# An encoder block's feed-forward entry: gate sums in another pool, low parts on VectorE, one token sum left in its PSUM bank

## The chip, the cores and the metric

The kernel runs on one core of one Trainium2 chip. The metric is the device time of one execution in microseconds; the median of three runs stands for a kernel. One further execution was recorded by the hardware profiler. Engines are named as the profile names them: PE is TensorE, DVE is VectorE, ACT is ScalarE, POOL is GpSimd, SP is the engine whose queue issues the DMAs.

## The reference

One layer of an encoder over 1024 tokens and 16 meta tokens, width 1024, in float32:

```python
h = concatenate([meta, x])
h = h + mixer_block(rms_norm(h, norm_mix), ...)      # two attention branches, gated, times w_out
h = h + swiglu(rms_norm(h, norm_ffn), w_ff_gate, w_ff_up, w_ff_down)
return rms_norm(h, norm_final)[:, N_META:]

def swiglu(h, w_gate, w_up, w_down):                 # inner width 2816
    return (silu(h @ w_gate) * (h @ w_up)) @ w_down
```

The change lies where the mixer's output has just been added to h and `h @ w_gate` and `h @ w_up` begin.

## The kernel before

**Split operands.** Each float32 operand of a matmul is kept as two parts, high and low. `split` (L110 to L112) makes them: ScalarE copies the source to the high part (L111), and a chosen engine subtracts that from the source for the low part (L112). A product of two split operands is three matmuls per 128 rows of depth: high by high, high by low, low by high.

**Seven products in place of eight.** The products with the gate's and the up's weights are done blockwise, 2 by 2, with seven products p = 1 to 7 in place of eight. `fp` (0 to 10) counts blocks of 256 inner columns, `i` is 0 for the gate and 1 for the up. The tokens' operands are b11, b21, b22 and, made of sums, t_5, t_6, t_7 and t_4. The weights' operands are made by `weights` (L903 on): p = 1 and 2 need only a raw block, p = 6, 5, 7 and 3 also sums of raw blocks (L918 to L924). p = 4 uses a raw block.

**The order.** `order_f` starts with p = 1 and 2 of the first three blocks (`N_EARLY = 3`), twelve products that do not need the tokens' sums; then follow p = 6, 5, 7, 3, 4 of these blocks, and then blocks 3 to 10 in full. TensorE's order is as written. The order on the other engines in this part is set by a planner, which plays the program through in a model and takes what is ready, the earlier written first. It also chooses the buffers, PSUM banks included; each engine then works its queue in that order.

**Products and banks.** `product_f` runs one product of 12 matmuls into a PSUM bank. There are eight banks. The bank that p = 1 opens (`b1`) is kept for p = 6, 7 and 4 of the same (i, fp); p = 2 has a bank of its own for a short time, and p = 5 and 3 share one. After p = 1 ScalarE copies the bank to a tile of the pool of copies (`p_tile`, 7 buffers, L1110). After p = 2 VectorE adds that copy to the bank: for the gate into a new tile c (L1099), to which ScalarE applies SiLU (L1101), for the up into the copy itself (L1104), after which c is multiplied by it (L1106). Tiles c come from `c_tile`: from a pool `cpool` of eight buffers, once that is open, before that from the pool of copies. `cpool` and `spool` are put where the pool of the h2 tiles was (`close_h2`), and that closes once the last token sums are split.

**Tokens' sums.** `norm_f(t)` normalises 128 tokens, `turn_f(t)` transposes them into two banks and splits them. For t = 4 to 7 it also makes four sums with the kept tiles of t - 4, u = t - 4 (L1023 to L1026): t1, t2, and two made in place of the kept tile (`left`, `low`), both from t2. `split_t(u)` then splits the four sums into t_6, t_5, t_7 and t_4, the last with its low part on POOL. `turn_f(6)` and `turn_f(7)` stand at the steps n = 0 and 2 of the loop over the products (`TURN`), the splits at n = 1, 3, 3 and 4 (`SPLIT`).

**Ahead of the products.** `prepare` makes weights' operands up to eight ahead; they live in a ring of eight (`op_tile`). Raw blocks come through a ring of five (`raw_tile`), which the normalised tokens and the weights of w_out use too. All loads and stores are issued from SP's queue in the planner's order, the stores of the h2 tiles (L995) among them.

Of the kernel before, what the change touches and what calls it, by code (L numbers as in the profile page):

```python
# [13 lines left out]
ALU = mybir.AluOpType  # L14
# [55 lines left out]
def encoder_block(ctx: ExitStack, tc: tile.TileContext, x, meta, norm_mix, w_in, lq1, lk1, lq2, lk2,  # L70
                  subln, sink, w_ba, w_bb, w_o, norm_ffn, w_g, w_u, w_d, norm_final, out, dbg=None):
    nc = tc.nc
# [5 lines left out]
    def f32(ap):  # L78
        return ap.bitcast(F32)
# [30 lines left out]
    def split(hi, lo, src, lo_eng):  # L110
        nc.scalar.activation(hi, src, AF.Copy)  # L111
        lo_eng.tensor_tensor(lo, src, f32(hi), ALU.subtract)  # L112
# [326 lines left out]
    for i in range(2):  # L439
        cols = slice(960 * i, 960 * i + 960)  # L440
# [293 lines left out]
    def ps_bank(name):  # L734
        return bank(psum3, "bank", name, 8)
# [5 lines left out]
    def op_tile(name):  # L741
        return ring.tile([P, 2, 512], F32R, tag="op", name=name, bufs=OP_BUFS)

    def raw_tile(name):
        return ring.tile([P, 1024], F32, tag="raw", name=name, bufs=RING_RAW)
# [23 lines left out]
    for j in range(4):  # L769
        nc.sync.dma_start(tb[:, 4 + j, :], yb_d[j])  # L770
        yb_t.append(ybpool.tile([P, 2, S], F32R, name=f"yb{j}"))
        if j % 2:
            for h in range(2):
                cols = slice(h * 512, h * 512 + 512)
# [70 lines left out]
    def half_op(p, name):  # L845
        return p.tile([P, 2, 4, 512], F32R, name=name)

    def h2_tile(name):
        return h2pool.tile([P, D], F32, tag="h2", name=name, bufs=NT)
# [17 lines left out]
    first, rest, order_pm = (1, 2), (6, 5, 7, 3, 4), (1, 2, 6, 5, 7, 3, 4)  # L867
    N_EARLY = 3
# [25 lines left out]
    def load_unit(i, fp, ahead=None):  # L894

        src = (w_g, w_u)[i]
        if ahead is not None:
            w = ahead.rearrange("p (c n) -> p c n", n=P)
            nc.sync.dma_start(w, src[:, fp * 256:fp * 256 + P].rearrange("(c p) n -> p c n", p=P))
            raws[i, fp, 0], raws[i, fp, 1] = w[:, 0:4], w[:, 4:8]  # L900
            return
        for kh in range(2):
            w = raw_tile(f"wf{i}_{fp}_{kh}").rearrange("p (c n) -> p c n", n=256)  # L903
            nc.sync.dma_start(w, src[kh * 512:kh * 512 + 512, fp * 256:fp * 256 + 256].rearrange("(c p) n -> p c n", p=P))
            raws[i, fp, kh] = w

    def weights(i, fp, p):
        if (p == 1 and fp) or (p == 6 and fp < N_EARLY):
            load_unit(i, fp, raw_tile(f"wf{i}_{fp}") if p == 1 and fp < N_EARLY else None)
        nm = f"{i}_{fp}_{p}"  # L910
        tt = nc.vector.tensor_tensor
        a11, a12 = (raws[i, fp, kh][:, :, 0:P] for kh in range(2))
        a21, a22 = (raws[i, fp, kh][:, :, P:256] for kh in range(2)) if p not in first else (None, None)
        src = {1: a11, 2: a12, 6: a11, 7: a21, 3: a12, 4: a22}.get(p)
        if p == 6:

            s1 = temps[i, fp] = spools[0].tile([P, 4, P], F32, tag="s", name=f"s1_{nm}", bufs=S_TMP)
            tt(s1, a21, a22, ALU.add)  # L918
            tt(a21, a11, a21, ALU.subtract)
            tt(a11, s1, a11, ALU.subtract)  # L920
        elif p == 5:
            src = temps[i, fp]
        elif p == 3:
            tt(a12, a12, a11, ALU.subtract)  # L924
        op = op_tile(f"wop_{nm}").rearrange("p a (c n) -> p a c n", n=P)
        split(op[:, 0], op[:, 1], src, nc.gpsimd)
        return op

    wt, late, raws_d = {}, [], {}
# [54 lines left out]
    def four(t):  # L984
        return t.rearrange("p (c t) -> p c t", c=4)

    xns, sums_t, held = {}, {}, {}
# [10 lines left out]
    def turn_f(t):  # L998
        xn = xns.pop(t)
        half, u = divmod(t, 4)  # L1000
        cols = slice(u * P, u * P + P)
        pts = []
        kept = None if half else h2_tile(f"kept_{u}")
        for b in range(2):
            pt = four(ps_bank(f"ptn_f{t}_{b}"))
            for c in range(4):
                k = 4 * b + c
                nc.tensor.transpose(pt[:, c, :], xn[:, k * P:(k + 1) * P], ident)
            pts.append(pt)
            if b or not half:  # L1010
                op = b22 if half else (b11, b21)[b]
                nc.scalar.activation(op[:, 0, :, cols], pt, AF.Copy)
                nc.vector.tensor_tensor(op[:, 1, :, cols], pt, f32(op[:, 0, :, cols]), ALU.subtract)
            if not half:
                nc.scalar.copy(four(kept[:, b * 512:b * 512 + 512]), pt)
        if not half:
            held[u] = kept
            return

        kept, more = held.pop(u), h2_tile(f"ts_{u}")  # L1020
        left, low = four(kept[:, 0:512]), four(kept[:, 512:])
        t1, t2 = four(more[:, 0:512]), four(more[:, 512:])
        nc.vector.tensor_tensor(t1, pts[0], left, ALU.subtract)  # L1023
        nc.vector.tensor_tensor(t2, pts[1], t1, ALU.subtract)
        nc.vector.tensor_tensor(left, t2, left, ALU.subtract)
        nc.vector.tensor_tensor(low, low, t2, ALU.subtract)  # L1026
        sums_t[u] = {5: t1, 6: t2, 7: left, 4: low}

    for i in range(2):
# [32 lines left out]
    t_ops = {p: half_op(topool, f"t_{p}") for p in (5, 6, 7, 4)}  # L1062
# [4 lines left out]
    def p_tile(name):  # L1067
        return pcopy.tile([P, 512], F32, tag="pc", name=name, bufs=P_BUFS)

    def c_tile(name):  # L1070
        return cpools[0].tile([P, 512], F32, tag="c", name=name, bufs=C_BUFS) if cpools else p_tile(name)

    def split_t(u):
        cols = slice(u * P, u * P + P)
        for p in (6, 5, 7, 4):
            split(t_ops[p][:, 0, :, cols], t_ops[p][:, 1, :, cols], sums_t[u][p], nc.gpsimd if p == 4 else nc.vector)

    st = {}

    def product_f(fp, p, i):  # L1080
        op, b = ops.pop(("f", (fp, p, i))), b_ops[p]
        u = st.setdefault((i, fp), {})
        nm = f"{i}_{fp}"
        which = {1: "b1", 6: "b1", 7: "b1", 4: "b1", 2: "b2", 5: "b3", 3: "b3"}[p]
        if p in (1, 2, 5):
            u[which] = ps_bank(f"pg_{nm}_{p}")
        ps = u[which]
        for c in range(4):
            for n, (x, y) in enumerate(((0, 0), (0, 1), (1, 0))):
                nc.tensor.matmul(ps, op[:, x, c, :], b[:, y, c, :], start=(p in (1, 2, 5) and c == 0 and n == 0),  # L1090
                                 stop=(p in (4, 2, 3) and c == 3 and n == 2), skip_group_check=True)
        g = st.setdefault(("c", fp), {})

        def result(key, src, other=None):

            if i == 0:
                c = g[key] = c_tile(f"c_{nm}_{key}")
                if other is not None:
                    nc.vector.tensor_tensor(c, src, other, ALU.add)  # L1099
                    src = c  # L1100
                nc.scalar.activation(c, src, AF.Silu)  # L1101
            else:
                if other is not None:
                    nc.vector.tensor_tensor(other, src, other, ALU.add)  # L1104
                    src = other
                nc.vector.tensor_tensor(g[key], g[key], src, ALU.mult)  # L1106

        if p in (1, 5):
            u[p] = p_tile(f"p{p}_{nm}")
            nc.scalar.copy(u[p], ps)  # L1110
        elif p == 6:
            u[p] = p_tile(f"u2_{nm}")
            nc.scalar.copy(u[p], ps)
        elif p == 2:
            result("11", ps, u[1])
        elif p == 7:
            result("22", ps, u[5])
        elif p == 3:
            result("12", ps, u[6])
        else:  # L1120
            result("21", ps)
            if i:

                a11, a21, a12, a22 = g["11"], g["12"], g["21"], g["22"]
                nc.sync.dma_start(a_d[1][fp], a11)
                s1, s2, s3, s4 = (c_tile(f"as{k}_{fp}") for k in range(1, 5))
                nc.vector.tensor_tensor(s1, a21, a22, ALU.add)
                nc.sync.dma_start(a_d[4][fp], a22)
                nc.vector.tensor_tensor(s3, a11, a21, ALU.subtract)
                nc.sync.dma_start(a_d[7][fp], s3)  # L1130
                nc.vector.tensor_tensor(s2, s1, a11, ALU.subtract)
                nc.sync.dma_start(a_d[5][fp], s1)
                nc.sync.dma_start(a_d[6][fp], s2)
                nc.vector.tensor_tensor(s4, a12, s2, ALU.subtract)
                nc.sync.dma_start(a_d[2][fp], a12)
                nc.sync.dma_start(a_d[3][fp], s4)

    TURN, SPLIT = {0: 6, 2: 7}, {1: (0,), 3: (1, 2), 4: (3,)}
    for n in range(nf):
        prepare()  # L1140
        if n in TURN:
# [97 lines left out]
    for n in range(nf, len(steps)):  # L1239
        p, j = steps[n][1]  # L1240
# [3 lines left out]
        if p in LOADS:  # L1244
            at, half, col = LOADS[p]
            if at <= j < at + 4:
                t, cols = 4 * half + j - at, slice(col * 512, col * 512 + 512)
# [60 lines left out]
```

## Time and profile before

| | |
|---|---|
| median of three runs | 1465.75 us (1465.35 to 1465.88) |
| profiled execution, its own time | 1464.45 us |
| its span, first to last instruction | 1462.7 us |
| granted clock of TensorE, mean | 0.999 |
| TensorE matmul, busy | 1437.6 us, 98% |
| VectorE, ScalarE, POOL busy | 863.2, 660.3, 542.3 us |
| gate and up products on TensorE (L1090) | from 820.0 to about 1244 us |

A row of a timeline begins with its start in us from the span's start, then its length, the engine, the line and the operation, output<-inputs, the tile's shape and how many instructions are merged; the bracket at its end gives the idle time before it and who ended it. A row of a group ends in busy us, the mean ns of one, and the idle time before. A row of a window gives the busy time of each engine in a stretch, with the number of instructions, then the granted clock, the share of DMA time and GB/s. An instruction that waits for a slot of a queue or a buffer has the same kind of bracket as one that waits for data.

### The profile page before, as it was taken

The numbers are of one execution on the slowest core, as the hardware profiler recorded it, in microseconds if no ns is written. First come the engines' busy times: TensorE is split into PE (matmuls) and PEld (weight loads), VectorE is DVE, ScalarE is ACT, GpSimd is POOL, SyncE is SP. The second block draws the span as 40 slices with busy tenths as digits, with TensorE's granted clock in tenths as the row PEclk, the third lists the DMA queues.
The fourth block names the chain that finished last, engine by engine and source line by source line (L and its number), as shares of the span: only waits on it lengthen the run. The fifth ranks groups of instructions, "written<-read, shape, count | busy, mean of one in ns | idle before, by whom it ended". The sixth has DMA issues, their size and how long they took to land.

```text
span 1462.7 us, 21039 instructions
## 1 busy us (share of the span) xinstructions
PE 1437.6 (98%) x7353; PEld 1237.7 (85%) x7353; DVE 863.2 (59%) x1664; ACT 660.3 (45%) x1245; POOL 542.3 (37%) x510
## 2 busy tenths in 40 slices
PE   6999999999999999999999999999999999999997
PEld 6989989988898999888888878888888888788886
DVE  6356426527786868533514886555555554787667
ACT  5365436525454545454515543333333333444454
POOL 4133223323323232224834566445454542000444
PEclk9999999999999999999999999999999999999999
DMA  7333343363524241086523434423333332964343
GB/s 234 89 98 114 110 125 101 77 199 102 147 79 146 73 152 67 29 274 215 176 106 130 144 108 138 135 96 103 99 108 101 104 101 98 337 204 142 124 125 142
DMA packets 157241, 192.06 MB, mean 131 GB/s; under 512 B 16256, under 2 KB 101696, under 8 KB 157136
## 3 DMA queue, kind: packets, MB, share of 16 engines
q1 hardware_dynamic: 157136, 190.73, 41.5%
q8 instruction: 58, 0.95, 0.3%
q14 instruction: 47, 0.39, 0.1%
HBM read 130.19 MB, written 53.94 MB: 126 GB/s over the span
## 4 chain that ended last, share of the span: by engine, by line
PE 84%; POOL 4%; issue 4%; DVE 3%; DMA 3%; ACT 1%; SPq 1%; POOLq 0%; DVEq 0%; ACTq 0%
PE pg L1090 27%; PE pp_g L199 10%; PE pd L1183 8%; PE po L860 6%; PE aps L588 4%; PE apy L630 3%; PE ppa L532 3%; PE pp_qb L199 3%; PE pp_va L199 3%; PE pp_qa L199 3%; PE pp_ka L199 3%; POOL oa L112 3%; PE apt L617 2%; PE bpt L337 2%; PE bpy L343 2%
## 5 line engine op out<-in xcount | busy, mean ns | idle before, releaser
L1090 PE MATMUL pg<-t,wop 128*128 128x512 f32 x1056 | 242.6, 389 | 0.0
L112 POOL TENSOR_TENSOR wop<-wf,wop 128x512 fp32r<-128x512 f32 x128 | 172.5, 1352 | 165.2 <-ACT wop L111 151.3
L1090 PEld LDWEIGHTS pg<-t,wop 128*128 128x128 f32 x1056 | 198.3, 188 | 41.1
L1183 PE MATMUL pd<-ob,oa 128*128 128x512 f32 x924 | 210.2, 389 | 1.3 <-DVE ob L112 0.9
L1183 PEld LDWEIGHTS pd<-ob,oa 128*128 128x128 f32 x924 | 173.3, 188 | 38.0 <-DVE ob L112 1.3
L1090 PE MATMUL pg<-b,wop 128*128 128x512 f32 x792 | 184.0, 390 | 3.2 <-DVE c L1099 2.8
L1090 PEld LDWEIGHTS pg<-b,wop 128*128 128x128 f32 x792 | 148.3, 188 | 35.0 <-issue 4.4
L112 POOL TENSOR_TENSOR wl_c<-w_c,wh_c 128x1024 fp32r<-128x1024 f32 x31 | 74.9, 2418 | 154.8 <-ACT wh_c L111 144.6
L111 ACT ACTIVATE wop<-wf 128x512 fp32r<-128x512 f32 x128 | 80.2, 631 | 83.8 <-PE pg L1090 48.2
L112 POOL TENSOR_TENSOR oa<-ra,oa 128x512 fp32r<-128x512 f32 x33 | 44.0, 1335 | 171.3 <-ACT oa L111 169.9
L599 ACT ACTIVATE as<-as,amn 128x1040 f32<-128x1040 f32 x64 | 74.5, 1165 | 72.8 <-DVE amn L594 72.8
L199 PE MATMUL pp_g<-hT_hi,wh_c 128*128 128x512 f32 x256 | 101.3, 396 | 0.0
L199 PE MATMUL pp_g<-hT_lo,wh_c 128*128 128x512 f32 x256 | 100.9, 394 | 0.0
L199 PE MATMUL pp_g<-hT_hi,wl_c 128*128 128x512 f32 x256 | 100.9, 394 | 0.0
L111 ACT ACTIVATE oa<-ra 128x512 fp32r<-128x512 f32 x77 | 48.7, 632 | 108.4 <-PE pd L1183 50.2
L588 PE MATMUL aps<-ak,aq 128*128 128x352 f32 (+1 forms) x384 | 92.6, 326 | 0.0
L860 PE MATMUL po<-woh,mT 128*128 128x512 f32 x384 | 88.6, 391 | 0.0
L918 DVE TENSOR_TENSOR s<-wf,wf 128x512 f32<-128x512 f32 x22 | 24.8, 1129 | 102.5 <-DMA wf<-in_w_ff_gate_dram 53.7
L860 PEld LDWEIGHTS po<-woh,mT 128*128 128x128 f32 x384 | 71.7, 188 | 14.7
L588 PEld LDWEIGHTS aps<-ak,aq 128*128 128x128 f32 x384 | 69.6, 188 | 14.0
L594 DVE CUSTOM_DVE_ANT_0 as<-aps,dist,amn 128x352 f32<-128x352 f32 (+1 forms) x128 | 71.3, 564 | 10.2 <-PE aps L588 8.2
L324 POOL TENSOR_SCALAR bs<-bs,bdn 128x432 f32<-128x432 f32 (+1 forms) x64 | 37.0, 596 | 95.6 <-DVE bdn L322 82.3
(249 smaller groups left out, 2965.1 us busy)
## 6 DMA issues: line engine op xcount, KB each, us to landing
ra<-aop SPq DMA_DIRECT2D x77, 256.0 KB, 2.7
w_c<-in_w_in_dram SPq DMA_DIRECT2D x33, 512.0 KB, 4.0
wf<-in_w_ff_gate_dram SPq DMA_DIRECT2D x24, 512.0 KB, 3.9
wf<-in_w_ff_up_dram SPq DMA_DIRECT2D x24, 512.0 KB, 3.8
aop<-as SPq DMA_DIRECT2D x44, 256.0 KB, 2.1
aop<-c SPq DMA_DIRECT2D x33, 256.0 KB, 2.0
g_d<-gate_stage SPq DMA_DIRECT2D x32, 256.0 KB, 2.0
gt<-g_d SPq DMA_DIRECT2D x32, 256.0 KB, 3.1
```

What stands on the lines that cost most here:

```text
L111: nc.scalar.activation(hi, src, AF.Copy)
L112: lo_eng.tensor_tensor(lo, src, f32(hi), ALU.subtract)
L199: nc.tensor.matmul(ps[:, :n], a[:, c, :], b[:, c, at:at + n], start=(c == 0 and i == 0), stop=(c == DC - 1 and i == 2))
L324: nc.gpsimd.tensor_scalar(st[:, r, :W], st[:, r, :W], dn[:, r:r + 1], 1.0, ALU.mult, ALU.mult)
L532: nc.tensor.matmul(ps, w[:, a, j, :], src(j, b, tk), start=(j == 0 and n == 0), stop=(j == 3 and n == 2))
L588: nc.tensor.matmul(ps[:, :n], qs[m][:, t * P:(t + 1) * P], ks[m][:, vv, k0:k0 + n], start=(vv == 0), stop=(vv == 1))
L594: nc.vector.tensor_tensor_reduce(s[m][:, a:b], ps[:, a - k0:b - k0], far_by, slope, low, ALU.add, ALU.min, mn[:, m, i + j:i + j + 1])
L599: nc.scalar.activation(s[m][:, 0:L], s[m][:, 0:L], AF.Exp, bias=low, scale=-1.0, accum_out=dn[:, m:m + 1])
L630: nc.tensor.matmul(py[:, cols], v[:kp, a, k, :], at_[:kp, k, b, :], start=(k == 0 and j == 0), stop=(k == 8))
L860: nc.tensor.matmul(ps, mT[:, c, a, t * P:(t + 1) * P], wos[q, c][:, b], start=(c == 0 and n == 0), stop=(c == DC - 1 and n == 2))
L1090: nc.tensor.matmul(ps, op[:, x, c, :], b[:, y, c, :], start=(p in (1, 2, 5) and c == 0 and n == 0), stop=(p in (4, 2, 3) and c == 3 and n ...
L1183: nc.tensor.matmul(ps[u], oa[:, a, u * P:(u + 1) * P], ob[:, b, :], start=(p in (1, 2, 5) and j == 0 and k == 0), stop=(p in (2, 3, 4) and ...
```

## The change

Four edits, all in the stretch around the first twelve products.

- In `weights`, the low parts for fp = 1 and 2, p = 1 and 2 (eight instructions) are made by VectorE, not POOL.
- In `turn_f`, the sum t2 overwrites the transposed bank from which it is made, in place of a half tile in SBUF. The next two sums read it there. For u = 0 and 1 ScalarE then copies it to the half tile, and the split reads that; for u = 2 and 3 the split reads the bank.
- In `split_t`, t_4's low part too is made by VectorE (four instructions). The splits stand earlier: u = 0 and 1 at n = 0, u = 2 at n = 1, u = 3 at n = 3.
- In `product_f`, the gate's tile c with key "11" comes from the pool of copies for fp = 0, 1 and 2. Before, only the first one did, since `cpool` was not open yet.

```diff
-        split(op[:, 0], op[:, 1], src, nc.gpsimd)
+        split(op[:, 0], op[:, 1], src, nc.vector if p in first and 0 < fp < N_EARLY else nc.gpsimd)
...
-        t1, t2 = four(more[:, 0:512]), four(more[:, 512:])
+        t1, t2 = four(more[:, 0:512]), pts[1]
         nc.vector.tensor_tensor(t1, pts[0], left, ALU.subtract)
-        nc.vector.tensor_tensor(t2, pts[1], t1, ALU.subtract)
+        nc.vector.tensor_tensor(t2, t2, t1, ALU.subtract)
         nc.vector.tensor_tensor(left, t2, left, ALU.subtract)
         nc.vector.tensor_tensor(low, low, t2, ALU.subtract)
+        if u < 2:
+            nc.scalar.copy(four(more[:, 512:]), t2)
+            t2 = four(more[:, 512:])
         sums_t[u] = {5: t1, 6: t2, 7: left, 4: low}
...
         for p in (6, 5, 7, 4):
-            split(t_ops[p][:, 0, :, cols], t_ops[p][:, 1, :, cols], sums_t[u][p], nc.gpsimd if p == 4 else nc.vector)
+            split(t_ops[p][:, 0, :, cols], t_ops[p][:, 1, :, cols], sums_t[u][p], nc.vector)
...
-                c = g[key] = c_tile(f"c_{nm}_{key}")
+                c = g[key] = (p_tile if key == "11" and fp < N_EARLY else c_tile)(f"c_{nm}_{key}")
...
-    TURN, SPLIT = {0: 6, 2: 7}, {1: (0,), 3: (1, 2), 4: (3,)}
+    TURN, SPLIT = {0: 6, 2: 7}, {0: (0, 1), 1: (2,), 3: (3,)}
```

## The prediction

> **What bounds the kernel now.** I read the page first, then TensorE's time by stage, then the timelines of the one stage in which it stands still.
>
> ```profile
> PE 1437.6 (98%) x7353; PEld 1237.7 (85%) x7353; DVE 863.2 (59%) x1664; ACT 660.3 (45%) x1245; POOL 542.3 (37%) x510
> ```
> ```profile
> core 0: us, PE busy (x) PEld busy (x) DVE busy (x) ACT busy (x) POOL busy (x), PEclk, DMA share, GB/s
> 800.00:820.00 20.00, 20.00 (x103) 16.85 (x101) 10.69 (x11) 6.02 (x11) 7.11 (x9) 1.00 0.19 79
> 820.00:840.00 20.00, 19.82 (x93) 16.26 (x92) 19.44 (x20) 15.47 (x29) 14.41 (x12) 1.00 0.78 211
> 840.00:860.00 20.00, 16.80 (x72) 13.01 (x71) 20.00 (x26) 8.33 (x15) 12.44 (x8) 1.00 0.26 79
> 860.00:880.00 20.00, 20.00 (x89) 16.55 (x89) 14.09 (x15) 8.69 (x16) 15.79 (x12) 1.00 0.41 118
> ```
> TensorE is busy 98% of the span. Everything that this change edits runs at the start of the gate and up products, and there TensorE lacks 0.18 us in the window from 820 and 3.20 us in the one from 840, at full granted clock. In the latter VectorE has not a moment free. In the windows before and after, TensorE runs without a gap, so 3.38 us is all that can be won here.
>
> I number the first twelve products n0 to n11: (fp 0) p1 p1 p2 p2, then for fp 1 and fp 2 p1, p2 with the gate's weights and p1, p2 with the up's. n12 is the first with p6. One product is 12 matmuls. The gaps in TensorE's timeline:
>
> ```profile
> 819.97 5.70 PE L1090 MATMUL pg<-b,wop 128*128 128x512 f32 x24
> 825.86 1.06 PE L1008 MATMUL ptn_f<-ident,xn_f 128*128 128x128 f32 x8 [0.18 <-DVE xn_f L994]
> 826.67 13.88 PE L1090 MATMUL pg<-b,wop 128*128 128x512 f32 x60
> 842.49 3.00 PE L1090 MATMUL pg<-b,wop 128*128 128x512 f32 x12 [1.93 <-DVE c L1099]
> 845.86 5.72 PE L1090 MATMUL pg<-b,wop 128*128 128x512 f32 x24 [0.38 <-DVE p L1104]
> 852.48 5.70 PE L1090 MATMUL pg<-b,wop 128*128 128x512 f32 x24 [0.89 <-DVE c L1099]
> 858.02 16.48 PE L1090 MATMUL pg<-t,wop 128*128 128x512 f32 x72
> ```
> n7 (842.49), n8 (845.86) and n10 (852.48) each wait for VectorE to release a PSUM bank by adding up an earlier product: n2, n3 and n5. These products were long finished: n2, the first of the five in the row at 826.67, ended about 826.67 + 13.88 / 5 = 829.4. VectorE was late because its queue was long:
>
> ```profile
> 834.87 6.87 DVE t L112 x4
> 841.74 0.60 DVE c L1099
> ```
> These are pieces of the chain that ended last: four low parts of the tokens' sums stand ahead of n2's addition.
>
> **VectorE's queue, before and after.** Why those four took 6.87 us:
>
> ```profile
> L112 DVE TENSOR_TENSOR t<-ts,t 128x512 fp32r<-128x512 f32 x8 | 9.6, 1213 | 0.0
> L1026 DVE TENSOR_TENSOR kept<-kept,ts 128x512 f32<-128x512 f32 x4 | 6.0, 1506 | 0.0
> L1025 DVE TENSOR_TENSOR kept<-ts,kept 128x512 f32<-128x512 f32 x4 | 4.9, 1232 | 0.0
> L112 DVE TENSOR_TENSOR t<-kept,t 128x512 fp32r<-128x512 f32 x4 | 4.9, 1230 | 0.0
> L1024 DVE TENSOR_TENSOR ts<-ptn_f,ts 128x512 f32<-128x512 f32 x4 | 2.7, 681 | 0.0
> ```
> ```profile
> 815.15 0.68 DVE L1024 TENSOR_TENSOR ts<-ptn_f,ts 128x512 f32<-128x512 f32 x1
> 819.10 1.76 DVE L1026 TENSOR_TENSOR kept<-kept,ts 128x512 f32<-128x512 f32 x1
> 820.79 0.67 DVE L865 TENSOR_TENSOR h<-h,po 128x512 f32<-128x512 f32 x1
> 841.66 0.68 DVE L1099 TENSOR_TENSOR c<-pg,p 128x512 f32<-128x512 f32 x1
> 842.26 1.16 DVE L112 TENSOR_TENSOR t<-ts,t 128x512 fp32r<-128x512 f32 x1
> 843.34 1.78 DVE L112 TENSOR_TENSOR t<-kept,t 128x512 fp32r<-128x512 f32 x1
> 845.04 0.68 DVE L1104 TENSOR_TENSOR p<-pg,p 128x512 f32<-128x512 f32 x1
> 846.24 0.68 DVE L1024 TENSOR_TENSOR ts<-ptn_f,ts 128x512 f32<-128x512 f32 x1
> 846.83 0.68 DVE L112 TENSOR_TENSOR t<-kept,t 128x512 fp32r<-128x512 f32 x1
> 847.43 0.68 DVE L112 TENSOR_TENSOR t<-ts,t 128x512 fp32r<-128x512 f32 x1
> 851.65 0.68 DVE L1099 TENSOR_TENSOR c<-pg,p 128x512 f32<-128x512 f32 x1
> 855.13 0.68 DVE L920 TENSOR_TENSOR wf<-s,wf 128x512 f32<-128x512 f32 x1
> ```
> ```profile
> 815.10 6.92 POOL L112 TENSOR_TENSOR wop<-first_f,wop 128x512 fp32r<-128x512 f32 x4 [0.17 <-ACT wop L111]
> 842.83 3.43 POOL L112 TENSOR_TENSOR wop<-wf,wop 128x512 fp32r<-128x512 f32 x2
> 856.61 3.26 POOL L112 TENSOR_TENSOR wop<-wf,wop 128x512 fp32r<-128x512 f32 x2 [3.75 <-ACT wop L111]
> ```
> One 128x512 VectorE instruction takes 0.68 us, and 0.60 from start to start (846.83 to 847.43). With both inputs in SBUF while POOL runs its own low parts it takes up to 1.78 (843.34, beside POOL's 842.83); with one input in PSUM it keeps 0.68 although POOL is running (815.15, beside POOL's 815.10). The four slow groups exceed 0.68 by 8x0.53 + 4x0.83 + 4x0.55 + 4x0.55 = 12.0 us.
>
> The Trainium skill ("SBUF — State Buffer", Who interferes with whom) says the same of a VectorE instruction with two SBUF inputs against a reading GpSimd one. But "Perfetto Trace Analysis" (Optimizing Scalar/DVE Operations) speaks against the change: if VectorE is saturated, give its work away, even to GpSimd; it adds that the shared port may spoil this. What the first half alone would give here is the last rival below.
>
> Part by part:
> - Low parts to VectorE: eight of the weights (fp 1 and 2, p 1 and 2) and four of the tokens' sums (p 4). 12 x 0.60 = 7.2 us are added to VectorE's queue, and from about 822 to 856 POOL has nothing big left, so all slow rows after 822 fall to 0.68.
> - t2 kept in its bank: L1025 and L1026 then have one PSUM input, and hold 0.68 even beside POOL's first four low parts, which stay. With the item above, all 12.0 us go. That VectorE writes PSUM (L1024's output) no row shows. Bounds: 0.68 as the same instruction into SBUF, or 1.78, the slowest row of this shape; four of them would add 4.4 us. I take 0.68, the nearest row; less than 0.68 no row of this shape has.
> - Two ScalarE copies, for u 0 and 1, take some 0.6 us each (the row at 849.89 below), on an engine with 4.5 of 20 us free. They can delay a token's low part, not the queue.
> - The earlier splits (u 0 and 1 at n0, u 2 at n1, u 3 at n3) only reorder what was in this queue anyway.
> - Gate sums "11" of fp 1 and 2 in the pool of copies: the same instruction, which no longer needs the space of the h2 tiles. VectorE shows no idle time for that now, so nought. The pool's seven buffers then hold three sums and four copies at most, which fits; if an earlier copy is still alive, ScalarE waits, not TensorE.
>
> Sum: 7.2 - 12.0 = -4.8 us on VectorE's queue. Does that reach each point at which TensorE waits? All times below are "ready in the old run", then shifted, against what TensorE would want without its gaps, taking all twelve additions as standing ahead.
> - n7's bank: 841.66 + 0.68 = 842.34; of the 12.0 us, 0.48 + 1.10 lie after it, so 842.34 - 10.4 + 7.2 = 839.1. Wanted at 842.49 - 1.93 - 0.18 = 840.4. Margin 1.2.
> - n8's: 845.72 - 4.8 = 840.9, wanted 845.86 - 2.49 = 843.4. Margin 2.4.
> - n10's: 852.33 - 4.8 = 847.5, wanted 852.48 - 3.38 = 849.1. Margin 1.6.
> - n12's weights, next in line: its low part on POOL ended at 856.61 + 1.63 = 858.24, and the third matmul of 858.02, its first user, came at about 858.48, so this is only just hidden now. It follows VectorE's L920 (855.13), so 853.4, wanted 858.48 - 3.38 = 855.1. Margin 1.7.
>
> So VectorE may stand idle 1.2 us in this stretch for nothing; each further microsecond W costs one: gain = 3.38 - (W - 1.2). What can make it idle is new: the weights' low parts now queue on VectorE, behind ScalarE's high parts, which wait for loads.
>
> ```profile
> 826.63 1.15 ACT L111 ACTIVATE wop<-wf 128x512 fp32r<-128x512 f32 x2 [2.95 <-DMA wf<-in_w_ff_gate_dram]
> 849.89 0.56 ACT L1110 COPY p<-pg 128x512 f32<-128x512 f32 x1
> ```
> ```profile
> 821.90 0.39 SPq L899 DMA_DIRECT2D wf<-in_w_ff_gate_dram  x1
> 824.84 1.60 SPq L899 DMA_DIRECT2D wf<-in_w_ff_up_dram  x1
> DMA to landing us min/median/max: 3.7/4.7/7.2
> ```
> The first of the four loads (821.90) stands on SP's queue behind the store of the last h2 tile, which waits for L865 (820.79). L1025 and L1026 of the first token block stand just ahead of L865, at 1.69 from start to start (819.10 to 820.79); at 0.60 each L865 comes 2.2 us sooner, at 818.6, and xn_f with it, so the 0.18 wait goes too. The load then lands near 821.9 - 2.2 + 4.7 = 824.4 instead of 826.6, while VectorE is still busy with the second block's sums. n4, the first user, starts at 826.67 + 2x2.78 = 832.2. I put W under 1.2.
>
> Forecast: nearly all of 3.38, say 3.2 us. The profiled execution took 1464.45 us (span 1462.7), the median of the runs is 1465.75; the same 3.2 off the median gives 1462.6.
>
> **Rivals.**
> - Another wait takes part of the place (chance 0.27). The second transposed bank of u 2 and u 3 is now held through L1025, L1026 and, as p6's source, through its two splits: about three to five instructions, 2 to 3 us, longer. At n7 all eight banks are in use: n0, n1, n4, n6 keep theirs, n2, n3, n5 and a transposed one fill the rest. Which bank a product gets is fixed by the planner, and it may name this one. For it: the margin at n7 is the smallest. Against it: its L1024 came only at 846.24 in the old order and is free to come sooner. Half of the gain stays: 1465.75 - 1.6 = 1464.2.
> - The change does not do what it says (0.13): the planner, which orders all engines but TensorE, sets n2's addition behind the new low parts and the earlier splits, or a PSUM write takes 1.78 and eats 4.4 of the 4.8 us. TensorE then waits as before: 1465.7. Against: every margin above already counts all twelve as ahead.
> - Head of the queue (0.12), the slower side: a low part whose load has not landed blocks VectorE. At W = 4.6 nothing is won, from W = 7.5 it is slower by over 0.2%. VectorE could reach them at about 822.3 (xn_f's place, less 2.2), and the last load issued until 826.4 may land 7.2 later, at 833.6: W up to 11.3. In the middle, at 9.4, it costs 4.8: 1470.5. Against it: a planner that knows loads puts other ready work first, and there is plenty.
> - The port is not relieved (0.04): the added 7.2 us then count in full on an engine without a free moment, n12's weights come 7.2 later with 0.24 to spare, and it ends at 1472.7. The rows at 846.83 and 847.43, both at 0.68 with POOL idle, speak against it. This is the outcome by the skill's page on trace analysis, saturated VectorE, without its reservation.
>
> **How the numbers follow.** A measurement here tells about 0.2% (2.9 us) from no change. The forecast has 0.44 and lies over that bound; rivals one and two (0.40) lie within it; three and four (0.16) are slower. Low end: 3.38 and 0.5 for the spread of the runs, 1461.9. The high end, 1467.5, takes in the case of no gain and a small loss, and leaves out the slower cases.
>
> **What would show it.** Right: in the new profile L1025, L1026 and the tokens' low parts at 0.68; no POOL row between about 823 and 852; TensorE without a gap from 820 to 860; L1024 into its bank at 0.68. Wrong: VectorE idle on a load or on ScalarE's wop before 835; a gap ahead of n4 to n10 that ends with a low part of weights or a split of u 2 or u 3; or any new gap after n12.

## The result, and the profile after

The changed kernel takes 1461.73 us in the median of 14 runs (1459.76 to 1464.64), the kernel before 1465.55 us in 14 runs beside it (1463.65 to 1468.3). The ratio is 0.9975, with a 95% interval from 0.9967 to 0.9983: 2.5 to 4.8 us less, 3.8 in the medians. The direction is the forecast one; the median lies 0.2 us below the low end of the range.

The profiled execution took 1459.76 us, its span is 1458.0 (1462.7 before). The page and TensorE's windows, as before:

```profile
PE 1436.3 (99%) x7353; PEld 1236.9 (85%) x7353; DVE 853.1 (59%) x1676; ACT 662.3 (45%) x1247; POOL 521.7 (36%) x498
```
```profile
820.00:840.00 20.00, 20.00 (x94) 16.64 (x93) 19.16 (x32) 15.38 (x29) 0.74 (x2) 1.00 0.74 217
840.00:860.00 20.00, 19.06 (x84) 15.29 (x83) 16.15 (x25) 10.75 (x21) 7.56 (x6) 1.00 0.21 67
```
POOL, busy 14.41 us in the first window before, is busy 0.74 us there; VectorE now has 3.85 us free in the second. TensorE's timeline shows the twelve early products without a break, and one gap inside n12, behind its second matmul (L1094 of the changed kernel is L1090 of before):

```profile
818.75 5.73 PE L1094 MATMUL pg<-b,wop 128*128 128x512 f32 x24
...
825.11 27.46 PE L1094 MATMUL pg<-b,wop 128*128 128x512 f32 x120
852.42 0.73 PE L1094 MATMUL pg<-t,wop 128*128 128x512 f32 x2
854.09 16.16 PE L1094 MATMUL pg<-t,wop 128*128 128x512 f32 x70 [0.94 <-POOL wop L112]
```

VectorE's groups from 811 to 856 us, the counterpart of the four slow ones:

```profile
L112 DVE TENSOR_TENSOR wop<-wf,wop 128x512 fp32r<-128x512 f32 x8 | 5.3, 688 | 0.8 <-ACT wop L111 0.8
L112 DVE TENSOR_TENSOR t<-kept,t 128x512 fp32r<-128x512 f32 x8 | 5.3, 687 | 0.1
L112 DVE TENSOR_TENSOR t<-ts,t 128x512 fp32r<-128x512 f32 x6 | 3.9, 688 | 0.0
L1025 DVE TENSOR_TENSOR ptn_f<-ptn_f,ts 128x512 f32<-128x512 f32 x4 | 2.8, 691 | 0.0
L1026 DVE TENSOR_TENSOR kept<-ptn_f,kept 128x512 f32<-128x512 f32 x4 | 2.7, 683 | 0.0
L1027 DVE TENSOR_TENSOR kept<-kept,ptn_f 128x512 f32<-128x512 f32 x4 | 2.7, 678 | 0.0
```
The slow rows of the four groups are gone. The write into PSUM (L1025) costs 0.69 us, as one into SBUF does. The only wait that VectorE got with the weights' low parts is 0.8 us, under the 1.2 that the prediction let pass.

The rows of matmuls hide a part of each gap; the rows of the weight loads (PEld) show it. Before:

```profile
842.46 2.61 PEld L1090 LDWEIGHTS pg<-b,wop 128*128 128x128 f32 x12 [2.33 <-issue]
845.83 5.33 PEld L1090 LDWEIGHTS pg<-b,wop 128*128 128x128 f32 x24 [0.77 <-issue]
852.45 5.31 PEld L1090 LDWEIGHTS pg<-b,wop 128*128 128x128 f32 x24 [1.28 <-issue]
```
and after:
```profile
854.09 5.99 PEld L1094 LDWEIGHTS pg<-t,wop 128*128 128x128 f32 x27 [1.38 <-POOL wop L112]
```
Each gap is 0.4 us longer here than in the matmul rows, whose last matmul before a gap is drawn 0.39 us long while the next would have started after 0.23. From the start of n0 to that of n12 there were 858.02 - 819.97 = 38.05 us, now 852.42 - 818.75 = 33.67: 4.4 us less, not 3.4. The gap in n12 takes 1.35 of that back. I call the time from the start of n0 to the first product of the down stage **the stretch**: 424.3 us before, 421.3 after, 3.0 less. Of the 4.7 us between the two spans, 1.2 lie ahead of n0 and 0.4 behind the stretch; the repeats below show how far such differences come from the single execution.

Ten kernels and six repeats follow; a "look" is one profiled execution. The stretch leaves out what varies ahead of n0 and is the finer measure, but most kernels have only one look. Ratios are of timed runs against the kernel before on the same chip. One of the ten timed runs of a_low took 1796.31 us at a mean granted clock of 0.755, and is left out of its ratio.

| kernel | stretch, us | gaps in it (matmul rows, us) | ratio, 95% interval |
|---|---|---|---|
| before, four looks | 424.3, 424.3, 427.0, 424.3 | n7 1.9, n8 0.4, n10 0.9 (2.0 in the third) | 1 |
| after, two looks | 421.3, 421.3 | n12 0.94 | 0.9975 (0.9967 to 0.9983), 0.9971 (0.9960 to 0.9981) |
| a_low | 422.3 | n12 0.54 and 0.94 | 0.9987 (0.9976 to 0.9998) |
| a_bank, two looks | 424.3, 424.3 | n9 2.1 | 0.9994 (0.9982 to 1.0006) |
| a_csum, two looks | 425.7, 425.7 | n7 1.9, n12 1.2; the second also n8 0.4, n11 0.7 | 1.0010 (1.0001 to 1.0020) |
| a_splt | 426.0 | n7 1.9, n8 0.4, n10 2.0, n12 0.3 | 1.0015 (0.9999 to 1.0031) |
| u_low | 421.8 | n9 1.6 | 0.9973 (0.9962 to 0.9985) |
| u_bank | 422.3 | n12 0.54 and 0.95 | 0.9978 (0.9967 to 0.9989) |
| u_csum | 421.8 | n9 0.5, n12 0.9 | 0.9969 (0.9955 to 0.9983) |
| u_splt | 421.3 | n12 0.94 | 0.9958 (0.9944 to 0.9972) |
| f_n12 | 421.9 | n12 1.6 | 0.9966 (0.9953 to 0.9979) |
| x_s1 | 420.4 | none | 0.9957 (0.9940 to 0.9973) |

### The profile page after: what moved, and what is told of

Its sections match the earlier page's. It is cut to its first block, busy times and chain, and to the rows that moved or that the text cites. A ratio compares the mean times of both kernels' runs of the same rounds, so it can differ in the third digit from the quotient of the medians.

```text
span 1458.0 us, 21027 instructions
## 1 busy us (share of the span) xinstructions
PE 1436.3 (99%) x7353; PEld 1236.9 (85%) x7353; DVE 853.1 (59%) x1676; ACT 662.3 (45%) x1247; POOL 521.7 (36%) x498
## 4 chain that ended last, share of the span: by engine, by line
PE 88%; issue 5%; POOL 4%; DMA 2%; DVE 1%; ACT 0%; SPq 0%; POOLq 0%; DVEq 0%; ACTq 0%
PE pg L1094 27%; PE pp_g L199 12%; PE pd L1188 8%; PE po L860 6%; PE aps L588 4%; PE apy L630 3%; PE ppa L532 3%; PE pp_ka L199 3%; PE pp_va L199 3%; PE pp_qb L199 3%; PE pp_qa L199 3%; POOL oa L112 3%; PE apt L617 2%; PE bpt L337 2%; PE bpy L343 2%
## 5 line engine op out<-in xcount | busy, mean ns | idle before, releaser
L1094 PE MATMUL pg<-t,wop 128*128 128x512 f32 x1056 | 243.0, 389 | 0.9 <-POOL wop L112 0.9
L1094 PEld LDWEIGHTS pg<-t,wop 128*128 128x128 f32 x1056 | 198.0, 188 | 42.7 <-POOL wop L112 1.4
L112 POOL TENSOR_TENSOR wop<-wf,wop 128x512 fp32r<-128x512 f32 x120 | 160.8, 1343 | 186.8 <-ACT wop L111 174.4
L1094 PE MATMUL pg<-b,wop 128*128 128x512 f32 x792 | 183.2, 389 | 0.0
L1094 PEld LDWEIGHTS pg<-b,wop 128*128 128x128 f32 x792 | 148.5, 188 | 30.8
L918 DVE TENSOR_TENSOR s<-wf,wf 128x512 f32<-128x512 f32 x22 | 16.3, 743 | 102.9 <-DMA wf<-in_w_ff_up_dram 52.2
```

## The experiments: each part alone

**The low parts alone.**
```diff
-        split(op[:, 0], op[:, 1], src, nc.gpsimd)
+        split(op[:, 0], op[:, 1], src, nc.vector if p in first and 0 < fp < N_EARLY else nc.gpsimd)
...
-            split(..., sums_t[u][p], nc.gpsimd if p == 4 else nc.vector)
+            split(..., sums_t[u][p], nc.vector)
```


> Only the twelve low parts go from POOL to VectorE; the rest is the kernel before. Measure: from the start of n0 to the start of the first product of the down stage (424.3 us before, 421.3 after). Theory 1, VectorE's queue: the slow rows behind 822 fall to 0.68 us (9.8 us less), 7.2 us are added, so the queue is 2.6 us shorter; L1025 and L1026 of the first block stay slow. The stretch shrinks by 1.5 to 2.6 us, to about 422.3, and some gap before n7 to n12 stays. Theory 2, the gain comes from the bank, the pool or the order: the stretch stays at 424 or grows, by up to 7 us, as VectorE has 7.2 us more.

422.3, as theory 1 had it: two thirds of the gain. The gaps before n7, n8 and n10 are gone, and n12 waits instead, first for ScalarE, then for POOL (TensorE's timeline of a_low):

```profile
853.43 0.73 PE L1090 MATMUL pg<-t,wop 128*128 128x512 f32 x2 [0.54 <-ACT wop L111]
855.11 5.07 PE L1090 MATMUL pg<-t,wop 128*128 128x512 f32 x21 [0.94 <-POOL wop L112]
```

**t2 in its bank alone.**
```diff
-        t1, t2 = four(more[:, 0:512]), four(more[:, 512:])
+        t1, t2 = four(more[:, 0:512]), pts[1]
-        nc.vector.tensor_tensor(t2, pts[1], t1, ALU.subtract)
+        nc.vector.tensor_tensor(t2, t2, t1, ALU.subtract)
...
+        if u < 2:
+            nc.scalar.copy(four(more[:, 512:]), t2)
+            t2 = four(more[:, 512:])
```


> Only t2 stays in its PSUM bank (with ScalarE's two copies). Theory 1, VectorE's queue: L1025 and L1026 keep 0.68 us beside a busy POOL, which takes 5.5 us out of the queue (4x0.55 and 4x0.83) and adds nothing; this alone then removes nearly all gaps before n7 to n12: the stretch goes from 424.3 to about 421. Theory 2, the relief of the port by an idle POOL is what counts: the low parts of the tokens' sums stay slow, and less than half of the gain is there, 422.8 or more.

The measured 424.3 lies in theory 2's range, and the tokens' low parts stay slow, as it said (groups of VectorE from 816 to 862 us, a_bank):

```profile
L112 DVE TENSOR_TENSOR t<-ts,t 128x512 fp32r<-128x512 f32 x6 | 8.3, 1404 | 1.1 <-ACT t L111 1.1
L112 DVE TENSOR_TENSOR t<-kept,t 128x512 fp32r<-128x512 f32 x4 | 4.9, 1221 | 0.0
```
But theory 1 has a share too: L1025 and L1026 hold 0.68 us, and the three old gaps are gone. What neither said is the new place of the loss: n9 now waits 2.1 us for the split that reads t2 of u 3 out of its bank (VectorE's row, then TensorE's, of a_bank):

```profile
851.31 0.68 DVE L112 TENSOR_TENSOR t<-ptn_f,t 128x512 fp32r<-128x512 f32 x1
```
```profile
852.14 10.04 PE L1093 MATMUL pg<-b,wop 128*128 128x512 f32 x36 [2.12 <-DVE t L112]
```
That is the held bank of the first rival. Behind this gap the granted clock is halved for 3.4 us (last section), which costs 1.7 us more; without that I estimate the stretch at 422.6, from 424.3 less 1.7.

**The gate sums alone.**
```diff
-                c = g[key] = c_tile(f"c_{nm}_{key}")
+                c = g[key] = (p_tile if key == "11" and fp < N_EARLY else c_tile)(f"c_{nm}_{key}")
```


> Only the gate sums of fp 1 and 2 come from the pool of copies. Theory 1: VectorE did not wait for the space of the h2 tiles, so the stretch stays within 0.4 us of 424.3. Theory 2: the third gap (0.89 us before n10) ended with such a sum, whose place was that of the h2 tiles; it goes, and the stretch is 1 us or more shorter.

The stretch is 1.4 us longer, in both looks, which neither theory said. The first look hides the later gaps behind a halved clock; the second shows them as they are (TensorE's timeline of the repeat):

```profile
854.74 3.02 PE L1090 MATMUL pg<-b,wop 128*128 128x512 f32 x12 [0.70 <-DVE p L1104]
857.60 0.61 PE L1090 MATMUL pg<-t,wop 128*128 128x512 f32 x2
859.49 10.76 PE L1090 MATMUL pg<-t,wop 128*128 128x512 f32 x46 [1.28 <-POOL wop L112]
```
The gap before n10 did end with the space of the h2 tiles: it is gone. But a gap before n11 and one in n12 came for it, since VectorE is still as late as before.

**The order of the splits alone.**
```diff
-    TURN, SPLIT = {0: 6, 2: 7}, {1: (0,), 3: (1, 2), 4: (3,)}
+    TURN, SPLIT = {0: 6, 2: 7}, {0: (0, 1), 1: (2,), 3: (3,)}
```


> Only the splits stand earlier (u 0 and 1 at n0, u 2 at n1, u 3 at n3). Theory 1: it reorders a queue whose length does not change; n2's addition comes no sooner, the stretch stays at 424.3 or grows by up to 1 us. Theory 2: the order alone brings part of the gain, 423 or less.

No gain, as theory 1 said, but 1.7 us more, over its bound of 1: the gap before n10 is 1.99 us. In this execution POOL got the port beside one of the last low parts of the tokens, as in the third look at before (below), so the order need not be the cause. Its eight timed runs have a median of 1467.59 us, against 1465.59 beside them; whether the order makes this likelier is open.

## The experiments: each part taken back

Each is the changed kernel with one part's diff reversed.

**Without the low parts.** 

> The changed kernel with the twelve low parts back on POOL. Theory 1, the low parts carry the change: tokens' splits on VectorE slow down to 1.2 to 1.8 us again, the twelve additions go, and gaps before n7 to n12 come back: between 422 and 424. Theory 2, the bank, the pool and the order are enough: 421.3 within 0.4.

421.8, with one gap, before n9. VectorE's low parts and a product's sum are slow again beside POOL, and n5's sum comes late (VectorE, then TensorE, of u_low):

```profile
843.24 2.95 DVE L112 TENSOR_TENSOR t<-ts,t 128x512 fp32r<-128x512 f32 x2
846.12 1.76 DVE L1109 TENSOR_TENSOR c<-c,p 128x512 f32<-128x512 f32 x1
847.81 0.68 DVE L1102 TENSOR_TENSOR c<-pg,p 128x512 f32<-128x512 f32 x1
```
```profile
848.54 8.45 PE L1093 MATMUL pg<-b,wop 128*128 128x512 f32 x36 [1.60 <-DVE c L1102]
```
Theory 1 had 422 to 424; the loss of 0.5 us is just outside of both theories. The low parts alone are worth 2.0 us, the three other parts together 2.5, all four 3.0: either relief does most of it.

**Without the bank.** 

> The changed kernel with t2 back in SBUF (no copies by ScalarE). Theory 1, VectorE's queue: L1025 and L1026 of the first block fall back to 1.7 us beside POOL's first four low parts, 2.2 us more in the queue, and L865 and the last xn_f come 2.2 us later; the gap before n12 grows, and the stretch from n0 to the down stage goes from 421.3 to between 422 and 423.5. Theory 2, the bank did nothing for the time: 421.3 within 0.4.

422.3, theory 1. It is the same stretch, with the same gaps, as with the low parts alone.

**Without the gate sums' pool.** 

> The changed kernel with the gate sums of fp 1 and 2 back in the pool that takes the place of the h2 tiles. Theory 1: nothing waits for that space, the stretch stays at 421.3 within 0.4. Theory 2: the sums of fp 1 then wait for the last token splits, VectorE holds their bank, and a gap of 0.5 to 2 us comes back before n9 to n11: 421.8 or more.

421.8: theory 2. A gap of 0.5 us comes before n9, which waits for n7's sum (TensorE's timeline of u_csum):

```profile
848.35 8.46 PE L1093 MATMUL pg<-b,wop 128*128 128x512 f32 x36 [0.47 <-DVE p L1107]
```
n5's sum now stands behind the last token split: it starts 28.6 us behind the start of n0, against 24.2 in the changed kernel, so n9 can't take its bank.

**Without the order of the splits.** 

> The changed kernel with the splits where they were (n1, n3, n3, n4). Theory 1: the same queue in another order, 421.3 within 0.4. Theory 2: the earlier splits are what lets VectorE do the low parts before the sums pile up; without them a gap before n7 to n12 comes back, 422 or more.

421.3: theory 1. The order does nothing for the time here, beside the other three.

## The experiments: the wait that is left

**Two more low parts on VectorE.**
```diff
-        ..., nc.vector if p in first and 0 < fp < N_EARLY else nc.gpsimd)
+        ..., nc.vector if (p in first and 0 < fp < N_EARLY) or (fp, p) == (0, 6) else nc.gpsimd)
```


> The changed kernel with two more low parts on VectorE, those of fp 0, p 6 (n12 and n13). The gap inside n12, the only one left in the stretch, ended with n12's low part on POOL (TensorE's row gives 0.94 us of idle time, the row of the weight loads 1.38). If the row of the weight loads is the true loss: 421.3 - 1.35 = 419.9. If the matmul row is: 420.3. If the sums of raw weights on VectorE (L918 to L920) are late in themselves, not POOL: 421 or more.

421.9, slower than the changed kernel. That is the third reading's number, but by another cause: the first L920 starts 32.3 us behind n0 in both kernels, and the planner put n12's low part behind three other instructions of VectorE (f_n12):

```profile
853.90 0.69 DVE L924 TENSOR_TENSOR wf<-wf,wf 128x512 f32<-128x512 f32 x1
854.50 0.69 DVE L1109 TENSOR_TENSOR p<-pg,p 128x512 f32<-128x512 f32 x1
855.10 0.69 DVE L924 TENSOR_TENSOR wf<-wf,wf 128x512 f32<-128x512 f32 x1
855.70 1.29 DVE L112 TENSOR_TENSOR wop<-wf,wop 128x512 fp32r<-128x512 f32 x2
```
It says nothing on the price of a gap; that was read from n0 to n12 above.

**s1 of fp 0 in another space.** In the changed kernel L918 stands right behind the last token split (VectorE, after):

```profile
847.41 0.68 DVE L112 TENSOR_TENSOR t<-kept,t 128x512 fp32r<-128x512 f32 x1
848.00 0.68 DVE L1104 TENSOR_TENSOR c<-pg,p 128x512 f32<-128x512 f32 x1
848.61 1.28 DVE L918 TENSOR_TENSOR s<-wf,wf 128x512 f32<-128x512 f32 x2
849.81 1.29 DVE L919 TENSOR_TENSOR wf<-wf 128x512 f32<-128x512 f32 x2
851.01 1.29 DVE L920 TENSOR_TENSOR wf<-s,wf 128x512 f32<-128x512 f32 x2
```
and its output lies where the h2 tiles were.
```diff
-            s1 = temps[i, fp] = spools[0].tile([P, 4, P], F32, tag="s", ...)
+            s1 = temps[i, fp] = (p_tile(f"s1_{nm}").rearrange("p (c n) -> p c n", n=P) if not fp else
+                                 spools[0].tile([P, 4, P], F32, tag="s", ...))
```


> The changed kernel, in which the first sum of raw weights (s1) of fp 0 takes a tile of the pool of copies in place of one that lies where the h2 tiles were. Theory 1: L918 waits for that space, that is for the last token split, and with it n12's weights; now they are some three VectorE instructions sooner (1.8 us), the gap in n12 (1.35 us of lost time) goes, and the stretch from n0 to the down stage falls from 421.3 to about 420. Theory 2: n12's low part on POOL is late because the chain of sums is long, not because it starts late: 421 or more.

420.4, theory 1. The same sum (now L919) runs 20.6 us behind the start of n0 in place of 29.9, ahead of the last token splits; n12's last sum (L921) runs at 30.2 in place of 32.3, and n12 follows n11 without a gap (VectorE, then TensorE, of x_s1, where n0 starts at 819.67):

```profile
840.30 0.68 DVE L919 TENSOR_TENSOR s<-wf,wf 128x512 f32<-128x512 f32 x1
...
849.91 0.68 DVE L921 TENSOR_TENSOR wf<-s,wf 128x512 f32<-128x512 f32 x1
```
```profile
826.03 27.95 PE L1095 MATMUL pg<-b,wop 128*128 128x512 f32 x120
853.82 16.48 PE L1095 MATMUL pg<-t,wop 128*128 128x512 f32 x72
```
Some 0.5 us went into two short waits before n12 in the weight loads' row. In timed runs it took 1460.54 us (four runs), the changed kernel beside it 1461.86 (ten runs), the kernel before 1466.4. It beats both in the median; against the changed kernel the intervals overlap, and the 0.9 us of the stretch, in one look, are what stands for it.

## The experiments: what the stretch does not hold

**The changed kernel again.** 

> The changed kernel once more, beside the two above on the same chip. The stretch from n0 to the down stage stays at 421.3 within 0.2; the start of n0 may move by a microsecond or more either way, since nothing ahead of it was changed, which would put the 1.2 us between the first two profiles there down to the single execution.

The stretch is 421.3 again, and n0 starts at 820.1, not at 818.75. The 1.2 us ahead of n0 were those of one execution: over all eighteen profiles n0 starts between 818.4 and 824.0, and the two looks at a_bank alone lie 2.8 us apart.

**The kernel before again, three times.** 

> The kernel before once more, one look. Two of the partial kernels had TensorE's granted clock at half for some 3.5 us behind a gap of 2.1 and 1.9 us. If such gaps bring this by chance, this execution may show it behind its own 1.9 us gap, and the stretch is then 426 in place of 424.3; if it doesn't, 424.3 within 0.2. The start of n0 moves freely.

> The kernel before, one more look. Gaps as before (1.93, 0.38, 0.89 us). Half clock by chance: it shows behind the 1.93 us gap in some execution, the stretch is then about 425 (the later gaps are swallowed in part). Half clock by program: never here, 424.3.

> As the look beside it: 424.3 without, about 425 with a half clock behind the 1.93 us gap.

Two looks give 424.3 with all gaps as they were; one gives 427.0. There the gap before n10 is 1.98 us. Beside the last token split POOL's and VectorE's low parts reach the port within 0.4 us of each other. In the first profile of before POOL's takes 2.79 us and VectorE's keeps its 0.68: VectorE holds the port and POOL waits (POOL's row, then VectorE's):

```profile
850.07 2.79 POOL L112 TENSOR_TENSOR t<-kept,t 128x512 fp32r<-128x512 f32 x1 [3.81 <-ACT t L111]
```
```profile
850.44 0.68 DVE L112 TENSOR_TENSOR t<-kept,t 128x512 fp32r<-128x512 f32 x1
```
In the third look POOL gets the port in between:

```profile
851.10 1.61 POOL L112 TENSOR_TENSOR t<-kept,t 128x512 fp32r<-128x512 f32 x1 [3.81 <-ACT t L111]
```
```profile
851.48 1.77 DVE L112 TENSOR_TENSOR t<-kept,t 128x512 fp32r<-128x512 f32 x1
```
n5's sum is then 1.1 us later, and the longer gap is followed by half a clock (the third look, by microseconds; the last figures but two are the granted clock):

```profile
854.00:855.00 1.00, 0.39 (x2) 0.38 (x3) 1.00 (x3) 0.46 (x1) 0.00 (x0) 1.00 0.65 227
855.00:856.00 1.00, 1.00 (x6) 0.83 (x5) 1.00 (x3) 0.65 (x2) 0.00 (x0) 0.99 0.07 16
856.00:857.00 1.00, 1.00 (x4) 0.73 (x4) 1.00 (x3) 0.00 (x0) 0.00 (x0) 0.50 0.00 0
857.00:858.00 1.00, 1.00 (x4) 0.81 (x3) 1.00 (x3) 0.46 (x1) 0.00 (x0) 0.50 0.00 0
858.00:859.00 1.00, 1.00 (x4) 0.81 (x3) 1.00 (x3) 0.43 (x2) 0.75 (x1) 0.50 0.05 20
859.00:860.00 1.00, 1.00 (x5) 0.78 (x5) 1.00 (x3) 1.00 (x3) 1.00 (x1) 0.80 0.64 242
```
Half a clock for 3.4 us loses 1.7 us: 1.1 us of waiting became 2.7 us of time. The changed kernel has no POOL work beside the tokens' splits and no gap above 1.38 us in the weight loads in this part, and neither look shows either loss.

**The two kernels with half a clock, again.** 

> Only the gate sums of fp 1 and 2 in the pool of copies, once more. By program: half clock again for 3 to 4 us behind the 1.93 us gap, stretch 425.7. By chance: without it, the gaps are seen as they are. If these sums waited for the h2 tiles' space, the gap before n10 is gone or smaller and the stretch about 424 to 424.3, with the gap in n12 in its place; if not, all gaps are those of before.

> Only t2 in its bank, once more. By program: half clock again behind the 2.1 us gap, stretch 424.2. By chance: without it the stretch is 424.2 - 1.7 = 422.5, or a little more if a wait that the slow clock covered now shows before n12.

a_csum came without half a clock, a_bank with it. So the program alone does not decide; the last section shows what does.

## Why the prediction was right or wrong, point by point

The main mechanism was forecast rightly. What failed are two sizes, the ceiling and above all the 0.5 us that the low end allows for the spread of the runs, and at n12 the assumption that VectorE's order stays.

- **The cause.** Right. Low parts on VectorE alone remove all three gaps, at twelve more instructions in its queue. The slow rows were POOL's doing: from 810 to 862 us of all eighteen profiles, no VectorE row of this shape is slow with an input in PSUM, and none with both inputs in SBUF unless one of POOL's low parts runs beside it. The Trainium skill's rule on the shared port ("SBUF — State Buffer", Who interferes with whom) agrees with these rows. Its sentence there that the order of issue decides who blocks can't be told from them: POOL's row begins 0.37 and 0.38 us ahead of VectorE's in the two looks above, while VectorE's instruction before it is still running, and once POOL won and once it didn't. The Trainium skill's half rule ("Perfetto Trace Analysis", Optimizing Scalar/DVE Operations), to give work away from a full VectorE, would have been wrong here, and its reservation about the port is what decides.
- **The ceiling of 3.38 us.** This step was mis-sized: it added up the idle time in front of matmul rows. The page of before had the true figure, 4.4 us, in a group of the weight loads, and n0 to n12 became 4.4 us shorter:

```profile
L1090 PEld LDWEIGHTS pg<-b,wop 128*128 128x128 f32 x792 | 148.3, 188 | 35.0 <-issue 4.4
```
- **The margin of 1.7 us at n12.** Wrong, and in the other direction: 1.35 us were lost there. TensorE came 1.0 us sooner than the ceiling allowed, and the weights some 1.8 us later than the shifted queue said. The sum assumed that VectorE's order stays. In fact the products' sums, no longer late, passed L918 (seven stand ahead of it, three before: 4 x 0.60 = 2.4 us), and L918 itself waits for the last split, for space (x_s1). Ceiling and margin offset each other: 4.4 - 1.35 = 3.0 in place of 3.2. That the sum came this near is luck.
- **The gate sums at nought.** Wrong in part: alone they cost 1.4 us, and in company they bring 0.6 (u_csum). That VectorE shows no idle time for a space says nothing, since the planner can order its queue by that space, as x_s1 shows for L918.
- **The bank held longer.** The rival came true only where t2 stays in its bank without the other parts (2.1 us before n9). In the changed kernel another wait did take part of the place, at n12, but by late weights and not by a bank.
- **PSUM write, ScalarE's copies, head of the queue.** Right for the changed kernel: 0.69 us, no wait, and 0.8 us of idle time.
- **The low end.** This is the step that failed for the time: 0.5 us below the full gain was taken from three runs that spread by 0.5 us, while fourteen runs of before spread by 4.7. The last 0.2 us are the base: before came out at 1465.55 us in fourteen runs, not 1465.75, and against that the gain of 3.8 us is within the 3.38 + 0.5 allowed. The prediction also put the chance part of the old kernel's own time at nothing. The stretch of the four looks at before averages 425.0, of the two after 421.3; the 3.7 us between them is close to the 3.8 of the medians, though four looks are few. The mean granted clock on record for each run points the same way: it is 0.998 or less in 42 of the 66 runs of before that have one, and in 8 of 24 of the changed kernel. But the runs at 0.999 alone still average 1465.6 and 1462.0 us, 3.6 apart where the stretch has 3.0. That the port's chance and the half clock make up the rest of the timed gain is thus likely and not shown.

## What to carry to other kernels

Price a gap of TensorE by the row of the weight loads, or by the time between two fixed matmuls; the matmul row hides 0.4 us of each gap. Moving work onto the fullest engine can shorten its queue, if the engine that gives it up slows the same queue through a shared port. When a queue is planned, a shift of its old order is no forecast: ask which instruction is held by space rather than by data, since that one stays. A single profile of a kernel with gaps shows one of its possible times: look at it more than once before taking a gain from it.

## What the runs showed of the hardware that was not expected

- TensorE's granted clock fell to 0.50 for 3.4 us, at most 1.4 us behind gaps of 2.33 to 2.52 us in the weight loads: in 4 of the 11 gaps of 2.28 us or more in this stretch, and behind none of the shorter ones. The Trainium skill ("TensorE: Matmul & The Clock Gate", HAM oscillation) warns of idle gaps over about 3.4 us; here less was enough, and the measurement decides.
- Which gaps bring it comes out of the traces' own times. In each of the eighteen executions the clock changed only at whole multiples of 3.413 us, counted from its first change; in the third look at before it changed at 19.72, at 855.99 (245 x 3.413 us later) and at 859.40. I cut each execution into such pieces and added up in each the time without a matmul row. Up to the last matmul, the clock was 0.50 behind every piece with 1.92 us or more of it, and behind none with 1.86 or less. In the four cases above one piece held 1.93, 1.98, 2.11 and 2.12 us; in each of the other seven gaps an edge divides the gap and leaves at most 1.86 us in one piece. u_bank has one more such spell outside the stretch, at 716.35, with 1.92 us in the piece. So the same gap costs up to 1.7 us more, or nothing, by where it falls among the pieces, and that moves from execution to execution.
- The port between VectorE and POOL makes one program's time a matter of chance: 1.77 or 0.68 us for the same instruction of the same kernel, by which engine got the port, with the rows 0.37 and 0.38 us apart.
